# Layer 0's feed-forward up half on one Trainium2 core: seven block products in place of eight, with some of the weights' sums made by DMA

## The chip, the cores and the metric

The kernel runs on one core of one Trainium2 chip. The metric is the device time of one execution in microseconds (us); three runs were timed, and their median counts. A further execution was recorded by the hardware profiler, and the trace is of that one.

## The reference

A diffusion backbone of two layers over 512 latent tokens (x) and 256 context tokens (ctx), model width 1024. Layer 0 mixes tokens by retention, layer 1 by differential attention; each is followed by a gated feed-forward with a convolution of three taps along the tokens. All is float32. Cut to what matters here:

```python
def rms_norm(x, g):
    y = x * lax.rsqrt(jnp.mean(x * x, axis=-1, keepdims=True) + EPS)
    return y * g

def modulate(xn, shift, scale):
    return xn * (1 + scale) + shift

def dwconv3(x, w, b):
    xp = jnp.pad(x, ((0, 0), (1, 1), (0, 0)))
    return xp[:, :-2] * w[0] + xp[:, 1:-1] * w[1] + xp[:, 2:] * w[2] + b

def conv_ffn(u, w_up, conv_w, conv_b, w_down):
    val, gate = jnp.split(u @ w_up, 2, axis=-1)
    return (jax.nn.silu(dwconv3(gate, conv_w, conv_b)) * val) @ w_down

for l in range(DEPTH):
    ...
    h_x = h_x + gm * rms_norm(yx, norm_g[l, 1])
    fx = conv_ffn(modulate(rms_norm(h_x, norm_g[l, 2]), shf, scf),
                  ffn_w_up[l], ffn_conv_w[l], ffn_conv_b[l], ffn_w_down[l])
    h_x = h_x + gf * rms_norm(fx, norm_g[l, 3])
    if not last:
        h_c = h_c + cgm * rms_norm(yc, norm_g[l, 1])
        fc = conv_ffn(modulate(rms_norm(h_c, norm_g[l, 2]), cshf, cscf), ...)
        h_c = h_c + cgf * rms_norm(fc, norm_g[l, 3])
```

The hidden width is 2816, or NF = 22 tiles of 128 (written f); `w_up` therefore has 44 units of 1024 x 128, two per f (gate and value). The shifts, scales and gates (adaLN) come from `silu(c) @ ada_w + ada_b`.

## The kernel before, in words

**Arithmetic.** Every fp32 product of the projections is made from three fp32r matmuls. An operand is split into a high part H (ScalarE copies it with rounding, L59) and a low part L (VectorE subtracts, L60); `split` is the function of both. `mm3` issues H by H, H by L and L by H on one PSUM bank (L97 to L99).

**Weights.** `W` loads a unit of 128x1024 by SP into one of three `wraw` buffers (`load_raw`, L64) and splits it into `wH`, `wL` (two buffers each) or into slots of the pools s2 or s6. The splits of weights and of loaded left operands run under `high_priority(offset=AHEAD)`: the scheduler that orders VectorE, ScalarE and POOL sets them ahead of work that was written up to 300 instructions earlier. SP and PE keep the order in which the code is written (`manual_schedule`).

**Pools.** s2: 48 slots of 128x512; s6: 8 slots of 128x1536; t2: 6 slots of 128x512 for short-lived tiles.

**Stages around the change.** Retention goes head by head: features of q and k (`feat`), projections of v and the gates (`proj_tok`), the two scans, and the result, transposed, goes to the DRAM tensor `yTd` by POOL's queue (`y_out`). `sublayer_out` then makes the output projection `ret_out` with 16 units k. Its **x half** takes tokens 0 to 3: per k SP loads the weights and 128x512 of `yTd`, and TensorE does 24 matmuls of 512 columns (4 tokens, 2 column halves, 3 products). Its **context half** takes tokens 4 and 5: 12 matmuls per k with weights loaded again up to two k ahead (`ahead`). Beside them a table `side` puts work at chosen k's: `fin` (gate, residual: L271, L274, tiles `ft` and `hn`), `keep` (store to DRAM), `sc` (the norm: `rstd_of` on ScalarE and POOL, then `xn` on VectorE), `tr` (16 transposes on TensorE, modulation and split into the operand `u` of the feed-forward, class `UT`).

**The up half** (`FFNUp`): per f, gate and value are each 8 k x 3 matmuls of 512 columns for x and as many of 256 for the context, that is 96 matmuls. `u` is the moving operand, the weights the stationary one. `conv` (L307 on) takes gate and value from PSUM: ScalarE scales and biases, VectorE adds the two neighbours (L323, L325), ScalarE does SiLU, VectorE multiplies by the value (L328). The hidden result stays in SBUF (`hTx`, `hTc`). Tiles 0 and 1 run their x parts first, since the context's tokens are done last:

```python
    F.run(0, 0, "x")
    F.run(0, 1, "x")
    ctx_part()
    F.run(1, 0, "x")
    ...
    F.rest(2)
```

**adaLN units.** 80 units (`ada_unit`): SP loads 128x1024 into `wraw`, VectorE does one or two multiply-reduces over it (L164). Nine per head lie in retention, two or three in a group (36); 44 lie in the up half, one behind each weight unit (`between`).

**The down half** is `sublayer_out` again, with 22 units and operands from SBUF. Layer 1 follows with the same pools.

## Time and profile before

| | |
|---|---|
| median of 3 runs | 2204.94 us (2198.9 to 2206.59) |
| profiled execution, its own time | 2202.28 us |
| its span in the trace | 2200.5 us |
| mean granted TensorE clock | 0.989 |
| TensorE (PE) busy | 2146.4 us, 98% of the span |
| VectorE (DVE) busy | 1222.3 us, 56% |
| ScalarE (ACT) busy | 843.8 us, 38% |
| GpSimd (POOL) busy | 242.5 us, 11% |
| DMA, mean | 114 GB/s |

Times in the trace are us from the span's start unless marked ns. PE is TensorE's matmul side, PEld its weight loads, which overlap. The ends of matmuls are modelled, so one matmul's shown duration overlaps the next; distances of starts tell what one costs. The runs' own time is 1.8 us above the span in the profiled execution. The up half of layer 0 lies between 876 and 1246 us, the x half of `ret_out` between 748 and 831, its context half from there to 877.

### The profile page before, as it was taken

What the parts mean: (1) busy time and instruction counts of PE and PEld (TensorE: products, weight loads), DVE (VectorE), ACT (ScalarE), POOL (GpSimd) and SP (SyncE); (2) the same over time, 40 slices, a digit from 0 to 9 for tenths busy, and PEclk for the clock granted to TensorE, in tenths of its full rate; (3) what the DMA queues carried; (4) which work ended last, traced back from release to release, by engine and by line L of the source; (5) the groups of instructions that cost most, each with busy time, mean ns of one, the idle gap of its engine ahead of it and who ended that gap; (6) DMA issues with size and microseconds to landing.
All of it is one profiled execution on the core that took longest, in us unless ns stands there. A gap on an engine that the chain in (4) does not pass through costs nothing. (4 is left out here: it accounts for less than half of the span.)

```text
span 2200.5 us, 28121 instructions
## 1 busy us (share of the span) xinstructions
PE 2146.4 (98%) x11096; PEld 1825.0 (83%) x11096; DVE 1222.3 (56%) x1923; ACT 843.8 (38%) x1488; POOL 242.5 (11%) x309
## 2 busy tenths in 40 slices
...
GB/s 269 100 92 87 130 86 68 121 86 67 101 96 101 115 220 200 140 116 143 129 124 128 146 105 196 212 44 47 43 45 30 115 114 117 98 99 98 108 96 125
DMA packets 82732, 250.68 MB, mean 114 GB/s; under 512 B 10104, under 2 KB 13480, under 8 KB 82472
## 3 DMA queue, kind: packets, MB, share of 16 engines
...
## 5 line engine op out<-in xcount | busy, mean ns | idle before, releaser
L60 DVE TENSOR_TENSOR wL<-wraw,wH 128x1024 fp32r<-128x1024 f32 x232 | 286.0, 1233 | 504.3 <-ACT wH L59 502.3
L59 ACT ACTIVATE wH<-wraw 128x1024 fp32r<-128x1024 f32 x257 | 271.5, 1058 | 646.1 <-PE psa L99 183.1
L97 PE MATMUL psf<-uxH,wH 128*128 128x512 f32 (+1 forms) x672 | 258.6, 385 | 0.0
L98 PE MATMUL psf<-uxL,wH 128*128 128x512 f32 (+1 forms) x672 | 258.5, 385 | 0.0
L99 PE MATMUL psf<-uxH,wL 128*128 128x512 f32 (+1 forms) x672 | 258.1, 384 | 0.1
L97 PE MATMUL pso<-wH,lxH 128*128 128x512 f32 x432 | 168.3, 390 | 0.5 <-ACT yo L579 0.3
L98 PE MATMUL pso<-wL,lxH 128*128 128x512 f32 x432 | 168.1, 389 | 0.0
L99 PE MATMUL pso<-wH,lxL 128*128 128x512 f32 x432 | 168.1, 389 | 0.0
L99 PEld LDWEIGHTS psf<-uxH,wL 128*128 128x128 f32 x672 | 126.3, 188 | 25.4 <-DVE wL L60 0.3
L97 PEld LDWEIGHTS psf<-uxH,wH 128*128 128x128 f32 x672 | 126.5, 188 | 24.0
L164 DVE CUSTOM_DVE_ANT_0 wraw<-wraw,cb 128x1024 f32<-128x1024 f32 x80 | 97.5, 1222 | 87.5 <-DMA wraw<-in_ada_rest_dram 86.8
L98 PEld LDWEIGHTS psf<-uxL,wH 128*128 128x128 f32 x672 | 126.5, 188 | 23.4
L97 PE MATMUL psa<-wH,uxH 128*128 128x512 f32 x352 | 137.0, 389 | 0.0
L98 PE MATMUL psa<-wL,uxH 128*128 128x512 f32 x352 | 137.0, 389 | 0.0
L99 PE MATMUL psa<-wH,uxL 128*128 128x512 f32 x352 | 136.9, 389 | 0.0
L137 POOL TENSOR_SCALAR st<-st 128x1 f32<-128x1 f32 x42 | 28.7, 684 | 682.3 <-ACT junk L136 681.1
L97 PEld LDWEIGHTS pso<-wH,lxH 128*128 128x128 f32 x432 | 81.1, 188 | 17.8 <-ACT grow L183 0.5
L99 PEld LDWEIGHTS pso<-wH,lxL 128*128 128x128 f32 x432 | 81.1, 188 | 17.0
L99 PE MATMUL psf<-ucH,wL 128*128 128x256 f32 x336 | 95.1, 283 | 0.0
L98 PE MATMUL psf<-ucL,wH 128*128 128x256 f32 x336 | 95.1, 283 | 0.0
L98 PEld LDWEIGHTS pso<-wL,lxH 128*128 128x128 f32 x432 | 81.1, 188 | 16.6
L97 PE MATMUL psf<-ucH,wH 128*128 128x256 f32 x336 | 94.9, 282 | 0.0
...
## 6 DMA issues: line engine op xcount, KB each, us to landing
wraw<-in_up_dram SPq DMA_DIRECT2D x88, 512.0 KB, 3.6
wraw<-in_ada_rest_dram SPq DMA_DIRECT2D x80, 512.0 KB, 3.7
wraw<-in_down_dram SPq DMA_DIRECT2D x66, 512.0 KB, 3.6
wraw<-in_ret_in_dram SPq DMA_DIRECT2D x64, 512.0 KB, 3.7
wraw<-in_ret_out_dram SPq DMA_DIRECT2D x32, 512.0 KB, 3.7
wraw<-in_diff_in_dram SPq DMA_DIRECT2D x24, 512.0 KB, 3.6
wraw<-in_ada_dram SPq DMA_DIRECT2D x16, 512.0 KB, 7.1
wraw<-in_diff_out_dram SPq DMA_DIRECT2D x16, 512.0 KB, 3.7
```

Source lines behind the costliest of these rows:

```text
L59: nc.scalar.activation(out=h, in_=x, func=AF.Copy)
L60: (eng or nc.vector).tensor_tensor(out=l, in0=x, in1=h.bitcast(F32), op=ALU.subtract)
L97: nc.tensor.matmul(ps, l[0], r[0], start=first, stop=False)
L98: nc.tensor.matmul(ps, l[0], r[1], start=False, stop=False)
L99: nc.tensor.matmul(ps, l[1], r[0], start=False, stop=last)
L137: nc.gpsimd.tensor_scalar(out=s[:, 2:3], in0=s[:, 0:1], scalar1=s[:, 1:2], scalar2=EPS, op0=ALU.add, op1=ALU.add)
L164: nc.vector.tensor_tensor_reduce(out=o, in0=raw, in1=cb[:, v, :], scale=1.0, scalar=0.0, op0=ALU.mult, op1=ALU.add, accum_out=adaF[:, laye ...
```

## The change

**Seven block products.** The product of the weights (gate and value; upper and lower half of the model width) with `u` (upper and lower half of the model width; even and odd blocks of 128 tokens) is a 2x2 by 2x2 block product. `seven_pass` makes it of seven block products in the order 1, 6, 7, 5, 2, 4, 3, each 4 k x 3 matmuls of 384 columns (256 of x, 128 of the context): 84 matmuls per f. Products 2, 3 and 4 have no bank of their own: their matmuls go on accumulating (`start=False`) on the banks of 1, 5 and 7. Between them ScalarE copies bank 1 to `p1`, and VectorE makes `u2` = bank 6 + p1, `u3` = bank 7 + u2, and from the banks of 5, 4 and 3 the value and the gate (L929). Tiles 0 and 1 are four passes: x of 0 and 1 (256 columns), then `ctx_part`, then the context of 0 and 1 (128 columns).

**Sums of the weights.** Each product needs its own stationary operand. `seven_load(f)` loads value's and gate's units; `sa` gets, by a plain DMA of SP, the upper halves of both, and then POOL's queue adds the value unit onto it in a DMA with `accum_op=add` (L901). It is issued two tiles ahead. `seven_w(f)` makes two further sums `sb` on VectorE (L912, L915) and splits seven operands (`wH`, `wL`, `opH`, `opL`), one tile ahead, under high priority.

**Sums of u.** Class `Seven` replaces `UT` there: `x_part(q)` (transposes, modulation, four sums and seven splits of 512 columns) at k = 6, 8, 10 and 12 of the context half; `ctx_part` the same for the context after tile 0's and 1's x passes. `seven_load` for tiles 0 and 1 is issued at k = 13, `seven_w(0)` at k = 14.

**The rest.** The hidden result goes to a DRAM tensor `hd` by POOL's queue and is loaded back in the down half (`load_y`), whose first two k's are loaded during tile 21. The adaLN units move: one behind every weight unit of `proj_tok` and every `feat` in retention (60), and the remaining 20 two ahead of each of the first ten k's of the x half of `ret_out`; none lies in the up half. s2 has 31 slots instead of 48, s6 16 instead of 8, and some tiles change pool.

```diff
-        return sp.tile(list(shape), dt, tag="s2", name=name, bufs=48)
+        return sp.tile(list(shape), dt, tag="s2", name=name, bufs=31)
...
-        return sp.tile(list(shape), dt, tag="s6", name=name, bufs=8)
+        return sp.tile(list(shape), dt, tag="s6", name=name, bufs=16)
...
@@ proj_tok, and after feat in retention
+            ada_next(1)
...
@@ retention
-            ada_next(2)
...
-        ada_next(3)
...
-        ada_next(2)
...
@@ sublayer_out
         for k in range(nk - 2):
-            w, lt = W(unit(k)), lx(k)
+            if seven:
+                ada_next(2)
+            w, lt = begun[k] if k < len(begun) else (W(unit(k)), lx(k))
...
-                    wcs.append(W(unit(j), "s6" if j % 2 == 0 else False))
+                    wcs.append(W(unit(j), j % 3 == 2 if seven else "s6" if j % 2 == 0 else False))
...
+        if seven:
+            side[13] = early
+            side |= {6 + 2 * q: lambda q=q: u.x_part(q, xn) for q in range(4)}
...
-            if k == nk - 1:
+            if k == nk - (2 if seven else 1):
                 first = pre()
...
+    ORDER = (1, 6, 7, 5, 2, 4, 3)
+    class Seven:
...
+        def sums(self, lo1, hi1, lo2, hi2, T, at):
+            a, b, c, d = T
+            stt = nc.vector.scalar_tensor_tensor
+            sub(a, lo1, hi1)
+            sub(b, hi2, hi1)
+            stt(out=c, in0=hi2, scalar=-1.0, in1=a, op0=ALU.mult, op1=ALU.subtract)
+            stt(out=d, in0=c, scalar=-1.0, in1=lo2, op0=ALU.mult, op1=ALU.subtract)
+            for i, x in ((1, lo1), (6, c), (7, b), (5, a), (2, lo2), (4, d), (3, hi2)):
+                split(at(self.H[i]), at(self.L[i]), x)
...
+    def seven_load(f):
...
+        nc.sync.dma_start(out=sa.rearrange("p (u c) -> p u c", u=2),
+                          in_=up[2 * f : 2 * f + 2, :, :512].rearrange("u p c -> p u c"))
+        g = load_raw(up[2 * f])
+        nc.sync.dma_start(out=v2, in_=up[2 * f + 1, :, 512:])
+        with tc.high_priority(offset=AHEAD):
+            nc.gpsimd.dma_start(out=sa, in_=up[2 * f + 1], accum_op=ALU.add)
...
+    def seven_w(loaded):
+        g, sa, v2 = loaded
+        with tc.high_priority(offset=AHEAD):
...
+            nc.vector.tensor_tensor(out=sb[0], in0=g[:, :512], in1=sa[:, 512:], op=ALU.add)
+            for i, x in ((6, sb[0]), (7, sa[:, :512]), (5, sa[:, 512:]), (4, v2), (3, sb[1])):
+                if i == 3:
+                    nc.vector.tensor_tensor(out=sb[1], in0=g[:, 512:], in1=sb[0], op=ALU.add)
+                H, L = s2(F32R, name="opH"), s2(F32R, name="opL")
+                split(H, L, x)
+                ops[i] = H, L
...
+    def seven_pass(f, u, ops, p, fp, after):
...
+        for i in ORDER:
+            on = {2: 1, 3: 5, 4: 7}.get(i)
+            banks[i] = banks[on] if on else bank("psf")[:, o]
+            ps = banks[i]
...
+            for k in range(4):
...
+                    nc.tensor.matmul(ps, a, b, start=on is None and k == 0 and j == 0, stop=k == 3 and j == 2,
+                                     skip_group_check=on is not None)
+            if i == 1:
+                after()
...
+        nc.gpsimd.dma_start(out=hd[f, :, s], in_=c[:, s])
...
+        seven_pass(0, u, ops[0], "x", fp, lambda: prepare(1))
+        seven_pass(1, u, ops[1], "x", fp, lambda: more(2))
+        ctx_part()
+        seven_pass(0, u, ops[0], "c", fp, lambda: None)
+        seven_pass(1, u, ops[1], "c", fp, lambda: (prepare(2), more(3)))
+        for f in range(2, NF):
+            seven_pass(f, u, ops[f], "all", fp, lambda: (prepare(f + 1), more(f + 2)))
```

**Where the order changes: VectorE and ScalarE at the start of the up half.** Before, VectorE, from the splits of the first up weights to the context's modulation (`ft`, `hn` and `xn` are tokens 4 and 5; `uf` and `ucL` the context's operand):

```order
L60 TENSOR_TENSOR wlL<-wraw,wlH 128x512 x4
L271 TENSOR_TENSOR ft<-pso,G 128x512 x3
L274 SCALAR_TENSOR_TENSOR hn<-ft,st,hin 128x512 x2
L271 TENSOR_TENSOR ft<-pso,G 128x512
L274 SCALAR_TENSOR_TENSOR hn<-ft,st,hin 128x512 x2
L220 TENSOR_SCALAR xn<-hn,st 128x512 x4
L60 TENSOR_TENSOR wL<-wraw,wH 128x1024 x2
L232 TENSOR_SCALAR uf<-pst,adaF 128x256
L60 TENSOR_TENSOR ucL<-uf,ucH 128x256
L232 TENSOR_SCALAR uf<-pst,adaF 128x256
L60 TENSOR_TENSOR ucL<-uf,ucH 128x256 x2
L232 TENSOR_SCALAR uf<-pst,adaF 128x256
```

After, VectorE at the same place, from the last two operands of tile 0 (`v_7241` is its `v2`; `sb`, `sa` and `v_7248` below `xn` are tile 1's; `u_7448` is pass 0's u2):

```order
L60 TENSOR_TENSOR opL<-v_7241,opH 128x512
L915 TENSOR_TENSOR sb<-wraw,sb 128x512
L60 TENSOR_TENSOR opL<-sb,opH 128x512
L277 SCALAR_TENSOR_TENSOR hn<-ft,st,hin 128x512 x4
L219 TENSOR_SCALAR xn<-hn,st 128x512 x4
L912 TENSOR_TENSOR sb<-wraw,sa 128x512
L60 TENSOR_TENSOR opL<-sb,opH 128x512
L60 TENSOR_TENSOR opL<-sa,opH 128x512 x2
L60 TENSOR_TENSOR opL<-v_7248,opH 128x512
L915 TENSOR_TENSOR sb<-wraw,sb 128x512
L60 TENSOR_TENSOR opL<-sb,opH 128x512
L929 TENSOR_TENSOR u_7448<-psf,p_7433 128x256
```

And ScalarE there in the change (`junk` is the square of the norm, `p_7433` pass 0's p1):

```order
L59 ACTIVATE opH<-sb 128x512
L59 ACTIVATE opH<-sa 128x512 x2
L59 ACTIVATE opH<-v_7241 128x512
L59 ACTIVATE opH<-sb 128x512
L136 ACTIVATE junk,st<-hn 128x512 x4
L183 ACTIVATE grow<-psg 8x128 x2
L59 ACTIVATE opH<-sb 128x512
L59 ACTIVATE opH<-sa 128x512 x2
L59 ACTIVATE opH<-v_7248 128x512
L59 ACTIVATE opH<-sb 128x512
L944 ACTIVATE p_7433<-psf 128x256
```

Tile 1's operands stand ahead of u2 on VectorE and ahead of p1 on ScalarE. On POOL the adding DMA of tile 2 (L901) stands ahead of two of the four steps (L137, L138) of tokens 4's and 5's norm.

**SP in the x half of `ret_out`.** Before, from the last units of retention (`G` is the gate row):

```order
L64 DMA wraw<-in_ret_in_dram 128x1024 x4
L64 DMA wraw<-in_ada_rest_dram 128x1024 x2
L191 DMA G<-gd 128x512 x2
L64 DMA wraw<-in_ret_out_dram 128x1024
L726 DMA yin<-yTd 128x512
L64 DMA wraw<-in_ret_out_dram 128x1024
L726 DMA yin<-yTd 128x512
```

After, from the last units of retention to the second k:

```order
L64 DMA wraw<-in_ret_in_dram 128x1024
L64 DMA wraw<-in_ada_rest_dram 128x1024
L191 DMA G<-gd 128x512 x2
L64 DMA wraw<-in_ada_rest_dram 128x1024 x2
L64 DMA wraw<-in_ret_out_dram 128x1024
L727 DMA yin<-yTd 128x512
L64 DMA wraw<-in_ada_rest_dram 128x1024 x2
L64 DMA wraw<-in_ret_out_dram 128x1024
L727 DMA yin<-yTd 128x512
```

Two adaLN loads now stand ahead of each k's weights, and the single ones lie between the weights of retention.

**VectorE in a steady pass** (f = 3 and later). Before, from one f's gate weights (the two L164 rows are an adaLN unit):

```order
L60 TENSOR_TENSOR wL<-wraw,wH 128x1024
L323 SCALAR_TENSOR_TENSOR conv<-psf,cw,conv 128x511
L325 SCALAR_TENSOR_TENSOR conv<-psf,cw,conv 128x511
L164 ISA adaj,adaF<-wraw,cb 128x1024
L164 ISA adaF 128x1
L164 ISA wraw,adaF<-wraw,cb 128x1024
L164 ISA adaF 128x1
L60 TENSOR_TENSOR wL<-wraw,wH 128x1024
L323 SCALAR_TENSOR_TENSOR conv<-psf,cw,conv 128x255
L325 SCALAR_TENSOR_TENSOR conv<-psf,cw,conv 128x255
L164 ISA adaj,adaF<-wraw,cb 128x1024
L164 ISA adaF 128x1
```

After, from u2 (`u_8009`) and u3 (`u_8024`) of a pass to its gate (`sb`, `sa`, `opL`, `wL` are the next tile's operands):

```order
L929 TENSOR_TENSOR u_8009<-psf,p_7994 128x384
L929 TENSOR_TENSOR u_8024<-psf,u_8009 128x384
L912 TENSOR_TENSOR sb<-wraw,sa 128x512
L60 TENSOR_TENSOR opL<-sb,opH 128x512
L929 TENSOR_TENSOR val<-psf,u_8024 128x3x128
L60 TENSOR_TENSOR opL<-sa,opH 128x512 x2
L60 TENSOR_TENSOR opL<-v_7988,opH 128x512
L915 TENSOR_TENSOR sb<-wraw,sb 128x512
L60 TENSOR_TENSOR wL<-wraw,wH 128x1024
L929 TENSOR_TENSOR val<-psf,u_8009 128x3x128
L60 TENSOR_TENSOR opL<-sb,opH 128x512
L929 TENSOR_TENSOR gate_8053<-psf,u_8009 128x3x128
```

The two adds for the value and the one for the gate stand among the next tile's splits; the adaLN units are gone from here.

## Rows read from the trace of the kernel before

**Rows 1.** The page: busy time, share of the span and instructions.
```profile
PE 2146.4 (98%) x11096; PEld 1825.0 (83%) x11096; DVE 1222.3 (56%) x1923; ACT 843.8 (38%) x1488; POOL 242.5 (11%) x309
```

**Rows 2.** Windows: us, then PE, PEld, DVE, ACT, POOL, PEclk, DMA share, GB/s.
```profile
831.00:877.00 46.00, 45.09 (x216) 37.14 (x215) 35.20 (x64) 31.15 (x67) 6.74 (x8) 1.00 0.61 208
...
905.00:1230.00 325.00, 325.00 (x1873) 287.66 (x1872) 175.58 (x273) 83.21 (x118) 0.00 (x0) 1.00 0.41 130
```

**Rows 3.** Tile psf: count, ns min/median/max, first and last start.
```profile
L97 PE MATMUL psf<-uxH,wlH x80: 277/283/474, 876.6 to 1861.2; 128*128 128x256 f32 x64, 128*128 128x512 f32 x16
...
L99 PE MATMUL psf<-ucH,wL x336: 283/283/283, 900.8 to 1245.3; 128*128 128x256 f32 x168
```

**Rows 4.** Timeline of PE: start us, duration us, instruction.
```profile
995.21 0.40 PE L97 MATMUL psf<-uxH,wH 128*128 128x512 f32 x1
...
1000.68 0.28 PE L97 MATMUL psf<-ucH,wH 128*128 128x256 f32 x1
...
1003.55 0.40 PE L97 MATMUL psf<-uxH,wH 128*128 128x512 f32 x1
```

**Rows 5.** Timeline of VectorE in the x half's end.
```profile
819.49 1.22 DVE L60 TENSOR_TENSOR wlL<-wraw,wlH 128x1024 fp32r<-128x1024 f32 x1
820.62 0.42 DVE L60 TENSOR_TENSOR lcHL<-yin,lcHL 128x256 fp32r<-128x256 f32 x1
820.96 1.28 DVE L271 TENSOR_TENSOR ft<-pso,G 128x512 f32<-128x512 f32 x2
822.16 1.40 DVE L274 SCALAR_TENSOR_TENSOR hn<-ft,st,hin 128x512 f32<-128x512 f32 x2
823.48 1.28 DVE L271 TENSOR_TENSOR ft<-pso,G 128x512 f32<-128x512 f32 x2
```

**Rows 6.** Timeline of ScalarE in the x half.
```profile
757.41 1.06 ACT L59 ACTIVATE wH<-wraw 128x1024 fp32r<-128x1024 f32 x1 [3.68 <-PE pso L99]
758.38 0.61 ACT L59 ACTIVATE lxH<-yin 128x512 fp32r<-128x512 f32 x1
```

**Rows 7.** DMA issues: tile, queue, count, KB, median us to landing; third row from 5 to 60 us.
```profile
wraw<-in_ret_out_dram SPq DMA_DIRECT2D x32, 512.0 KB, 3.7
...
yTd<-yo POOLq DMA_DIRECT2D x16, 256.0 KB, 4.8
...
wraw<-in_ada_dram SPq DMA_DIRECT2D x14, 512.0 KB, 7.8
```

**Rows 8.** Timeline of PE: transposes in the context half, plain fp32 at the start.
```profile
841.54 1.91 PE L242 MATMUL pst<-ident,hn 128*128 128x128 f32 x16
843.21 0.48 PE L97 MATMUL pso<-wH,lcHL 128*128 128x512 f32 x1
...
1.11 5.29 PE L424 MATMUL warm<-ones 128*128 128x128 f32 x26 [1.11 <-DVE etile L125]
6.33 1.89 PE L381 MATMUL psada<-wraw,csil 128*2 128x256 f32 x8
```

**Rows 9.** Timeline of VectorE at the start of the up half.
```profile
876.25 1.88 DVE L271 TENSOR_TENSOR ft<-pso,G 128x512 f32<-128x512 f32 x3
...
884.38 0.88 DVE L220 TENSOR_SCALAR xn<-hn,st 128x512 f32<-128x512 f32 x2 [1.35 <-POOL st L138]
```

**Rows 10.** Windows around an idle stretch of PE in layer 1.
```profile
1725.00:1730.00 5.00, 0.65 (x2) 0.58 (x3) 4.81 (x11) 1.76 (x5) 0.00 (x0) 0.50 0.55 157
1730.00:1735.00 5.00, 5.00 (x23) 4.22 (x22) 0.59 (x2) 1.06 (x1) 0.55 (x1) 0.73 0.00 0
```

**Rows 11.** Timeline of SP in the context half.
```profile
857.48 0.33 SPq L64 DMA_DIRECT2D wraw<-in_ret_out_dram  x1
...
863.69 0.33 SPq L64 DMA_DIRECT2D wraw<-in_ret_out_dram  x1
```

More of the change, by code (lines that the diff above doesn't have):

```diff
@@ L357, in lhs_c @@
         return at
+    cbs = tc.tile_pool(name="cbs", bufs=1)
+    cb = cbs.__enter__().tile([P, 2, 1024], F32, name="cb")
     l0 = tc.tile_pool(name="l0", bufs=1)
@@ L481, in first_ctx @@
     def first_ctx():
-        U.add_ctx()
         norm_pair(psp, U, "c", xs[4:6], 0, 0)
@@ L720, in tile_hybrid_backbone, with load_y @@
         prev_y = yg
-    def load_y(lo, hi):
+    def load_y(src, lo, hi):
         def at(k):
             y = s2(name="yin")
-            nc.sync.dma_start(out=y[:, : hi - lo], in_=yTd[k, :, lo:hi])
+            nc.sync.dma_start(out=y[:, : hi - lo], in_=src[k, :, lo:hi])
             return y[:, : hi - lo]
@@ L730, in tile_hybrid_backbone, with sublayer_out @@
     rows = lambda a, t: a[t * P : (t + 1) * P, :]
-    def sublayer_out(nk, unit, lx, lc, chunk, prev, dst_x, dst_c, layer, sub_i, hook, pre):
+    def sublayer_out(nk, unit, lx, lc, chunk, prev, dst_x, dst_c, layer, sub_i, hook, pre, seven=False, early=None, begun=()):
         G = load_gate(0, chunk, 0)
@@ new lines, in modulated_on @@
+    def modulated_on(uf, ps, k, v, act):
+        a, b = adaF[:, 0, v, 4, k : k + 1], adaF[:, 0, v, 3, k : k + 1]
+        if act:
+            nc.scalar.activation(out=uf, in_=ps, func=AF.Identity, scale=a, bias=b)
+        else:
+            nc.vector.tensor_scalar(out=uf, in0=ps, scalar1=a, scalar2=b, op0=ALU.mult, op1=ALU.add)
+    def seven_load(f):
+        up = A["up"][0]
+        sa = s6(name="sa")[:, :1024]
+        v2 = s2(name="v2")
+        nc.sync.dma_start(out=sa.rearrange("p (u c) -> p u c", u=2),
[4 more added lines that the diff above has]
+            nc.gpsimd.dma_start(out=sa, in_=up[2 * f + 1], accum_op=ALU.add)
+        return g, sa, v2
@@ new lines, in seven_w @@
+    def seven_w(loaded):
+        g, sa, v2 = loaded
+        with tc.high_priority(offset=AHEAD):
+            H, L = wp.tile([P, 1024], F32R, tag="wH", name="wH", bufs=2), wp.tile([P, 1024], F32R, tag="wL", name="wL", bufs=2)
+            split(H, L, g)
+            ops = {1: (H[:, :512], L[:, :512]), 2: (H[:, 512:], L[:, 512:])}
+            sb = [s2(name="sb") for _ in range(2)]
+            nc.vector.tensor_tensor(out=sb[0], in0=g[:, :512], in1=sa[:, 512:], op=ALU.add)
[5 more added lines that the diff above has]
+                ops[i] = H, L
+        return ops
@@ new lines, in ffn0, with more, prepare @@
+    def ffn0(u, loads, ops, ctx_part, then):
+        pool = tc.tile_pool(name="ff", bufs=1)
+        fp = pool.__enter__()
+        end = []
+        def more(f):
+            if f < NF:
+                loads.append(seven_load(f))
+        def prepare(f):
+            if f < NF:
+                ops.append(seven_w(loads[f]))
+            else:
+                end.extend(then())
+        seven_pass(0, u, ops[0], "x", fp, lambda: prepare(1))
[5 more added lines that the diff above has]
+            seven_pass(f, u, ops[f], "all", fp, lambda: (prepare(f + 1), more(f + 2)))
+        pool.__exit__(None, None, None)
+        return end
@@ L818, in tile_hybrid_backbone @@
+    hd = dr.tile([NF, P, 768], F32, name="hd")
+    loads = []
     u, ctx_part, first = sublayer_out(
-        16, lambda k: A["ret_out"][k], lhs_x(load_y(0, 512)), lhs_c(load_y(512, 768)), 2, tok_src,
-        lambda t: rows(h1d, t), lambda t: rows(h1d, t), 0, 1, lambda: y_out(3, prev_y), pre_up)
+        16, lambda k: A["ret_out"][k], lhs_x(load_y(yTd, 0, 512)), lhs_c(load_y(yTd, 512, 768)), 2, tok_src,
+        lambda t: rows(h1d, t), lambda t: rows(h1d, t), 0, 1, lambda: y_out(3, prev_y), lambda: seven_w(loads[0]), True,
+        lambda: loads.extend(seven_load(f) for f in range(2)))
@@ L821, in tile_hybrid_backbone @@
     flush_rows(psp)
-    F = FFNUp(psp, u, 0, True, ada_next)
-    F.w[0, 0], F.w[0, 1] = first
-    F.run(0, 0, "x")
-    F.run(0, 1, "x")
-    ctx_part()
-    F.run(1, 0, "x")
-    F.conv(0, "x")
-    F.run(0, 0, "c")
-    F.run(0, 1, "c")
-    F.run(1, 0, "c")
-    F.conv(0, "c")
-    for p in ("x", "c"):
-        F.run(1, 1, p)
-    F.conv(1, "x")
-    F.conv(1, "c")
-    F.rest(2)
+    l0.__exit__(None, None, None)
+    down, hx = lambda k: A["down"][0, k], lhs_x(load_y(hd, 0, 512))
+    begun = ffn0(u, loads, [first], ctx_part, lambda: [(W(down(0)), hx(0)), (W(down(1), True), hx(1))])
@@ L1052, in part @@
                 yield
-    acc = {}
+    acc, acct = {}, {}
     def evac(t, n, ps):
-        acc[t, n] = s2(name="acc")
+        if t not in acct:
+            acct[t] = s6(shape=(P, 3, 512), name="acc")
+        acc[t, n] = acct[t][:, n, :]
         with tc.high_priority(offset=20):
```

139 lines of the change are left out of this document (109 added, 30 removed).

## The prediction

> **What bounds the kernel now.** I read the page's busy times first: TensorE is busy for 2146.4 of 2200.5 us [rows 1], so the kernel ends when its matmuls are through. Then the windows by stage [rows 2]: in the stretch of layer 0's up half (905 to 1230) TensorE is busy throughout, VectorE 175.58 of 325 us, at full clock; nothing but TensorE can be made shorter there. The tile view of `psf` gives the stage's ends, 876.6 and 1245.3 [rows 3]: 368.7 us. The matmuls overlap, so their price is the distance of their starts: 24 of 512 columns take 5.47 us (995.21 to 1000.68), 24 of 256 take 2.87 (1000.68 to 1003.55) [rows 4], that is 0.228 and 0.1196 each. One tile f has 48 of each, 16.68 us; f = 2 to 21 take 333.6, and the stage's first two tiles with the context's transposes the other 35.1.
>
> The profiled execution took 2202.28 us, 2.66 below the median of the three runs (2204.94). The sum is made against 2202.3; the forecast is left at the sum, since one execution cannot say which of the two a new run will be nearer.
>
> **Tiles f = 2 to 21: the gain.** The change takes 7 x 4 x 3 = 84 matmuls of 384 columns in place of 96. No row has 384 columns; the two prices of [rows 4] lie on a straight line of 0.1084 us per 256 columns, so 0.174, with ends 0.1196 and 0.228. I take the middle: 14.60 us a tile, 2.08 less, over 20 tiles **-41.6 us**. (The ends would be 10.0 and 19.2 us a tile; a price that fell on either would break the line that the two points make, so they don't widen the range.)
>
> This holds if VectorE and ScalarE stay ahead. VectorE's prices are distances of starts [rows 5]: 1.13 us for a 128x1024 split, 0.34 for 256 columns, 0.60 for 512 (ft, from PSUM), 0.66 for a three-operand one of 512. Per tile: 7 sums and splits of 512 (4.2), one of 1024 (1.13), 5 adds of 384 from PSUM (2.35, between 0.34 and 0.60 each), four convolution steps (2.1) and the last product of 768 (0.95): 10.7 of 14.6 us. Today it is 175.58/325 of 16.68, or 9.0 us. ScalarE: 1.06 and five times 0.6 [rows 6], two copies, two convolution steps, some 6.8. In the order of instructions the adds that free the banks of products 7 and 5 come before the splits that wait longest; u3 is due when product 4 starts, 10.4 us into a pass, and stands at about 7.6; val's first add is due at 12.5 and stands at about 10. So I cost the shared banks at nothing; VectorE's slack of some 2.5 us covers them.
>
> The sums by DMA: per tile 512 KB plain and 512 KB added, beside 768 KB of weights and 384 KB of `hd`, 2.2 MB in 14.6 us, 155 GB/s where the stretch now moves 130 [rows 2]. No row has an adding DMA. Nearest: POOL's 256 KB stores land in 4.8 us, SP's 512 KB loads in 3.7, in the crowded start 7.8 [rows 7]. Twice the store's, 9.6 us, is my value, 3.7 the low end; there is no row for a high one. It has about 20 us: `sa` of tile f+2 lands at the start of pass f-1 and is first read some 7.6 us into pass f. At nothing.
>
> **Tiles 0 and 1: a loss.** They run as four passes: 84 matmuls of 256 columns twice (10.0 us each), and 84 of 128 twice. For 128 columns the nearest row is the transposes, 16 in 1.67 us, 0.104 each; the dearest is the plain fp32 matmul of the same shape, 26 in 5.22 us, 0.20 [rows 8]. I take 0.104, as the loads of the stationary operand have the same shape in both: 8.8 us a pass (16.9 at the upper end). The Trainium skill (TensorE: Matmul & The Clock Gate, "Back-to-back issue gap") gives about 81 ns per 128-column matmul with its weight load; the 168 would then cost 3.9 us less. The same sentence gives 131 ns for 512 columns, where the rows above show 228, so I go by the rows.
>
> Waits come on top. Count from the end of the context's products (876.6 in the trace), in VectorE's order as the fences show it: the last ft at 2 us [rows 9]; tile 0's operands, 7 x 0.60 and twice 0.6 of waiting for ScalarE, to 8; hn to 10.5; xn not before 14, because on POOL the two steps of its rstd stand behind tile 2's adding DMA, that waits for a load (3.7 us) which waits for tile 0's `sa` to be read (at 5.5). Today xn is done 8.7 us after the same point. Then tile 1's operands, to 19.7; only then u2 and u3 of pass 0, to 20.5. Product 2 waits for p1, which ScalarE has behind tile 1's splits, and product 4 for u3; TensorE is through products 1, 6, 7 and 5 by 9, idles about 10 us, and ends pass 0 at 24 instead of 10. Pass 1 ends at 34, the transposes at 36. The context's sums (4 modulations, 4 sums, 7 splits of 512 and pass 1's convolution, 10 us) let product 6 start at 45.5; six products of 1.25 us end at 53, the last pass at 61.8. Today: 35.1. **+27 us** (lower end +10, if the order's waits come out at a third; upper +43 with 0.20 for 128 columns). While TensorE idles the clock may fall: the trace shows 0.50 in 1725 to 1730, in which PE was busy for 0.65 us of 5, and 0.73 in the next 5 [rows 10]. Some 3 us at half speed lose **+2** (0 to 5).
>
> **Output projection of retention, x half.** 20 adaLN units move here, two ahead of each of 10 k's loads on SP. With three `wraw` buffers each k now turns all three, and W(k+1)'s load starts only when W(k) is split. The trace's fastest turn of one buffer is 6.21 us (857.48 to 863.69, two issues between) [rows 11]; from its parts, 3.7 landing, 1.06 and 1.13 splits, 0.3 issue, 6.2 too. TensorE needs a k every 24 x 0.228 = 5.47. Ten times 0.75 less some 3 us that W is ahead at the start: +4.5; with landings slower, since three units of 512 KB and one of 256 KB every 6.2 us are 290 GB/s, a k every 7 us and +12. I take **+7** (0 to 20). The 24 units moved into retention's projections and features cost nothing: one unit beside each W every 8 us is what the up half does today without a stall [rows 2]; if that cover were gone, VectorE would be late with evacuations, not TensorE with columns.
>
> **Output projection, context half.** VectorE gains 4 x (11 x 0.34 + 0.46) = 16.8 for the seven sums, and loses 16 x 0.34 + 8 x 0.45 = 9.0: 7.8 us more, where it is busy for 35.2 of 46 today [rows 2]; with operands that wait for ScalarE between the two splits I take **+5** (0 to 12).
>
> `hd`'s stores (POOL) and its loads back (SP, 256 KB beside 512 KB per k) are hidden as retention's `yTd` is, in the same loop; without that cover each k would be late by a landing. The changed buffer counts leave layer 1's order nearly as it was: 0 (-5 to +5).
>
> **Sum:** 2202.3 - 41.6 + 27 + 2 + 7 + 5 = 2201.7, say **2202 us**. A measurement of this kernel tells about 0.5% (11 us) from no change: faster is below 2194, slower above 2216.
>
> **Rivals.**
> 1. *The waits at the stage's start are mostly hidden* (faster). For it: TensorE has most of products 1, 6, 7, 5 to run, and the x half may keep its lead through 10 k's. Then start +16, projections +3 together, clock 0: 2180, up to 2192. Against: an in-order VectorE cannot take u2 before tile 1's operands.
> 2. *128-column matmuls cost what plain fp32 ones do* (slower). 168 x (0.20 - 0.104) = +16, and with the x half at 7 us a k another +5: 2223. It decides from 0.19 us each. For it: plain fp32 is the only non-transposing 128-column row; against it, its operands are plain fp32.
> 3. *The adding DMA is late* (slower). Beyond 20 us from issue to landing each pass waits for it; at 25 us that is 5 us a pass, +100: 2300. For it: no row bounds it. The Trainium skill (DMA: Bandwidth & Descriptors, "SWDGE vs HWDGE vs iDMA") says that GpSimd writes such a DMA's descriptors into SBUF, and that VectorE can lock it out meanwhile. By that rule it would be later the busier VectorE is; no row here shows POOL's DMAs beside a VectorE busy at 73%.
> 4. *The change saves no columns*: 84 matmuls at 0.228 would be 19.2 us a tile, +52: 2295. Both prices of [rows 4] speak against it; a chance within that of case 3.
>
> **Chances.** Forecast 0.35, rival 1 0.33, rival 2 0.27, rivals 3 and 4 0.05. Faster 0.33, same 0.35, slower 0.32. The cases reach from 2180 to 2223; with the ends of the terms beside them and no more than 0.2 left out, the range is 2178 to 2235. The forecast's own range is 2192 to 2214.
>
> **What would show it.** Right: in the middle of the stage 84 matmul starts about 0.174 us apart and a pass of 14.6 us; one idle stretch of TensorE of about 10 us just after the context's products, ended by ScalarE's p1 or VectorE's u3, and one before product 6 of the first context pass; k's of 6.2 us in the first ten of the x half, with the two splits of W as releasers. Wrong: passes longer than 15 us with an `sa` DMA as releaser (rival 3); 128-column starts 0.2 apart (rival 2); no idle stretch above 5 us at the stage's start (rival 1); or new waits in layer 1.

## The result: 1.4% slower, and where the time went

The changed kernel takes 2233.56 us (2231.60 to 2234.95, four runs) against 2204.53 us of the kernel before: a ratio of 1.0136, interval 1.0120 to 1.0151. The forecast was 2202, no change. The profiled execution took 2231.60 us. The first lines of the profile's page, to be read beside [rows 1]:

```profile
span 2229.8 us, 28616 instructions
PE 2139.8 (96%) x11000; PEld 1854.1 (83%) x11000; DVE 1355.4 (61%) x2180; ACT 905.0 (41%) x1588; POOL 283.1 (13%) x354
```

TensorE has 96 matmuls less and 6.6 us less busy time, yet the span is 29.3 us longer: it now stands idle or runs slowly somewhere. The windows by stage say where (us, then PE, PEld, DVE, ACT, POOL, PEclk, DMA share, GB/s). Before, the x half and tiles 0 and 1 ([rows 2] has the context half and the later tiles):

```profile
736.60:827.90 91.30, 90.48 (x409) 74.61 (x408) 38.43 (x49) 35.04 (x55) 7.71 (x16) 1.00 0.58 196
...
876.60:911.70 35.10, 35.10 (x211) 31.23 (x209) 24.71 (x45) 16.45 (x38) 6.35 (x10) 1.00 0.40 136
```

After, in order: x half of the output projection, its context half, pass 0, pass 1, the two context passes, tile 2, tiles 3 to 20.

```profile
741.20:844.50 103.30, 95.50 (x409) 76.08 (x408) 59.56 (x88) 36.39 (x59) 8.56 (x16) 0.97 0.77 261
844.50:894.40 49.90, 48.12 (x226) 39.15 (x225) 47.34 (x95) 37.78 (x85) 14.70 (x11) 1.00 0.76 247
894.50:925.00 30.50, 14.71 (x86) 14.09 (x85) 19.38 (x34) 11.89 (x28) 7.51 (x12) 0.72 0.60 177
925.00:939.10 14.10, 12.06 (x102) 11.82 (x101) 7.26 (x14) 5.50 (x11) 1.52 (x2) 1.00 0.37 85
939.10:961.70 22.60, 18.44 (x84) 18.07 (x85) 14.48 (x26) 8.25 (x15) 1.43 (x2) 0.53 0.29 93
961.70:979.60 17.90, 17.90 (x86) 17.90 (x86) 8.19 (x16) 5.22 (x10) 1.43 (x2) 0.50 0.45 114
979.70:996.50 16.80, 16.80 (x85) 16.80 (x85) 9.16 (x16) 5.78 (x10) 0.57 (x1) 0.85 0.41 104
996.60:1258.00 261.40, 261.40 (x1510) 261.40 (x1509) 199.21 (x320) 118.78 (x179) 23.98 (x34) 1.00 0.53 148
```

The stages run from the first matmul of one to the first of the next:

| stage | before, us | changed, us | difference | forecast |
|---|---|---|---|---|
| all before the x half | 736.6 | 741.2 | +4.6 | 0 |
| x half of `ret_out` | 91.3 | 103.3 | +12.0 | +7 |
| its context half | 48.7 | 49.9 | +1.2 | +5 |
| tiles 0 and 1 of the up half | 35.1 | 85.2 | +50.1 | +29 (with the clock's +2) |
| tiles 2 to 21 | 333.6 | 293.6 | -40.0 | -41.6 |
| all after the up half | 955.1 | 956.6 | +1.5 | 0 |

**The steady passes came as forecast.** The first matmuls of two neighbouring passes:

```profile
1011.13 0.33 PE L939 MATMUL psf<-tH,wH 128*128 128x384 f32 x1
...
1025.69 0.33 PE L939 MATMUL psf<-tH,wH 128*128 128x384 f32 x1
```

14.56 us for 84 matmuls, 0.1733 each, in each of 19 tiles; VectorE is busy for 199.21/261.40 of that, 11.1 us (10.7 forecast). No pass waits for a bank, a sum or a DMA.

**Pass 0 waits twice.** TensorE's timeline, from the last matmul of product 1 to the first of product 2 (in brackets: idle time before, and what ended it); then VectorE's and ScalarE's rows that stand behind it:

```profile
895.86 0.28 PE L939 MATMUL psf<-tH,wL 128*128 128x256 f32 x1
...
901.54 0.58 PE L939 MATMUL psf<-tH,opH 128*128 128x256 f32 x1 [5.41 <-ACT opH L59]
...
908.01 0.28 PE L939 MATMUL psf<-tH,opL 128*128 128x256 f32 x1
...
918.66 0.58 PE L939 MATMUL psf<-tH,wH 128*128 128x256 f32 x1 [10.38 <-ACT p L944]
```

```profile
898.41 1.23 DVE L60 TENSOR_TENSOR wL<-wraw,wH 128x1024 fp32r<-128x1024 f32 x1 [1.16 <-ACT wH L59]
...
900.15 0.68 DVE L912 TENSOR_TENSOR sb<-wraw,sa 128x512 f32<-128x512 f32 x1
...
912.40 0.88 DVE L219 TENSOR_SCALAR xn<-hn,st 128x512 f32<-128x512 f32 x2 [1.35 <-POOL st L138]
...
913.20 0.68 DVE L912 TENSOR_TENSOR sb<-wraw,sa 128x512 f32<-128x512 f32 x1
...
918.98 0.42 DVE L929 TENSOR_TENSOR u<-psf,p 128x256 f32<-128x256 f32 x1
```

```profile
897.32 1.06 ACT L59 ACTIVATE wH<-wraw 128x1024 fp32r<-128x1024 f32 x1 [1.76 <-DMA wraw<-in_up_dram]
...
900.86 0.63 ACT L59 ACTIVATE opH<-sb 128x512 fp32r<-128x512 f32 x1 [1.91 <-DVE sb L912]
...
917.71 0.63 ACT L59 ACTIVATE opH<-sb 128x512 fp32r<-128x512 f32 x1 [1.60 <-DVE sb L915]
918.24 0.37 ACT L944 ACTIVATE p<-psf 128x256 f32<-128x256 f32 x1
```

Product 6 waits 5.41 us for `opH` of tile 0 (ScalarE 900.86). That stands behind `wH` and `wL` of tile 1 (897.32, 898.41), which waited for tile 1's load. That order is not the whole of it: tile 0's adding DMA, issued at 887.11, took 9.3 us from issue to landing, so its sum, which begins at 900.15, could not have begun before some 896.4. Product 2 waits 10.38 us for p1 (918.24), which stands behind tile 1's operands (the last at 917.71); u2 follows at 918.98, behind tokens 4's and 5's `xn` and tile 1's sum (913.20) and its splits.

**The context passes run at half clock.** In 961.70 to 979.60 TensorE is busy without a gap and yet has a granted clock of 0.50, the 1.2 GHz level; 128 columns cost 0.213 us there:

```profile
961.74 0.41 PE L939 MATMUL psf<-tH,wH 128*128 128x128 f32 x1
961.95 0.41 PE L939 MATMUL psf<-tL,wH 128*128 128x128 f32 x1
```

### The profile page after: what moved, and what is told of

It reads as the page before. It is cut to its first block, busy times and chain, and to the rows that moved or that the text cites. A ratio compares the mean times of both kernels' runs of the same rounds, so it can differ in the third digit from the quotient of the medians.

```text
span 2229.8 us, 28616 instructions
## 1 busy us (share of the span) xinstructions
PE 2139.8 (96%) x11000; PEld 1854.1 (83%) x11000; DVE 1355.4 (61%) x2180; ACT 905.0 (41%) x1588; POOL 283.1 (13%) x354
## 3 DMA queue, kind: packets, MB, share of 16 engines
q0 software_dynamic: 7744, 28.08, 5.1%
## 5 line engine op out<-in xcount | busy, mean ns | idle before, releaser
L97 PE MATMUL psa<-wH,u 128*128 128x512 f32 x528 | 205.7, 390 | 0.4 <-DVE ptmp L659 0.4
L98 PE MATMUL psa<-wL,u 128*128 128x512 f32 x528 | 205.5, 389 | 0.0
L99 PE MATMUL psa<-wH,u 128*128 128x512 f32 x528 | 205.4, 389 | 0.0
L939 PE MATMUL psf<-tH,opH 128*128 128x384 f32 (+2 forms) x480 | 163.3, 340 | 5.4 <-ACT opH L59 5.4
L939 PE MATMUL psf<-tL,opH 128*128 128x384 f32 (+2 forms) x480 | 163.0, 340 | 2.5 <-DVE tL L60 2.5
L939 PE MATMUL psf<-tH,opL 128*128 128x384 f32 (+2 forms) x480 | 163.0, 340 | 0.0
L99 PE MATMUL psf<-u,wL 128*128 128x512 f32 (+1 forms) x336 | 127.4, 379 | 0.2 <-DVE wL L60 0.2
L97 PE MATMUL psf<-u,wH 128*128 128x512 f32 (+1 forms) x336 | 127.3, 379 | 0.0
L98 PE MATMUL psf<-u,wH 128*128 128x512 f32 (+1 forms) x336 | 127.3, 379 | 0.0
L164 DVE CUSTOM_DVE_ANT_0 wraw<-wraw,cb 128x1024 f32<-128x1024 f32 x80 | 97.3, 1219 | 36.7 <-DMA wraw<-in_ada_rest_dram 36.0
L97 PEld LDWEIGHTS psa<-wH,u 128*128 128x128 f32 x528 | 99.1, 188 | 21.6 <-DVE ptmp L659 1.3
L99 PEld LDWEIGHTS psa<-wH,u 128*128 128x128 f32 x528 | 99.1, 188 | 20.6
L98 PEld LDWEIGHTS psa<-wL,u 128*128 128x128 f32 x528 | 99.1, 188 | 20.2
L137 POOL TENSOR_SCALAR st<-st 128x1 f32<-128x1 f32 x42 | 33.2, 790 | 641.2 <-ACT junk L136 639.2
L939 PEld LDWEIGHTS psf<-tH,opH 128*128 128x128 f32 x480 | 97.7, 204 | 5.7 <-ACT opH L59 5.6
```

The source lines that it names most:

```text
L97: nc.tensor.matmul(ps, l[0], r[0], start=first, stop=False)
L98: nc.tensor.matmul(ps, l[0], r[1], start=False, stop=False)
L99: nc.tensor.matmul(ps, l[1], r[0], start=False, stop=last)
L137: nc.gpsimd.tensor_scalar(out=s[:, 2:3], in0=s[:, 0:1], scalar1=s[:, 1:2], scalar2=EPS, op0=ALU.add, op1=ALU.add)
L164: nc.vector.tensor_tensor_reduce(out=o, in0=raw, in1=cb[:, v, :], scale=1.0, scalar=0.0, op0=ALU.mult, op1=ALU.add, accum_out=adaF[:, laye ...
L939: nc.tensor.matmul(ps, a, b, start=on is None and k == 0 and j == 0, stop=k == 3 and j == 2, skip_group_check=on is not None)
```

## The experiments

My theory after the result had three parts: the clock in the context passes, the order on VectorE and ScalarE in pass 0, and the adaLN units in the x half. Kernels that share a stage's instructions still differ by some us in it, so I read each edit in its own stage. Except where an edit is said to be on the kernel before, it is on the changed kernel.

### Narrow matmuls at full clock

```diff
+    CUTS = {8: ((0, 256), (256, 384)), 14: ((0, 128), (128, 256), (256, 384))}
...
-                    nc.tensor.matmul(ps, a, b, ...)
+                    for c0, c1 in CUTS.get(f if p == "all" else None, ((0, n),)):
+                        nc.tensor.matmul(ps[:, c0:c1], a, b[:, c0:c1], ...)
```

> The changed kernel with two tiles cut into narrower matmuls in the middle of the steady stretch, where the granted clock is 1.00: tile 8 does each 384-column matmul as 256 and 128 columns, tile 14 as three of 128. Question: why did the two context passes take 17.9 us where 8.8 were forecast. Theory A (their price belongs to the clock, 0.50 in that stretch; at full clock a 128-column matmul costs half of 0.213): tile 8's pass takes 84 x (0.120 + 0.107) = 19.0 us; tile 14's pass 252 x 0.107 = 27.0 us if the clock stays full in a stream of 128-column matmuls, and up to 53.7 us if such a stream itself lets the granted clock fall to 0.50. Theory B (128 columns cost 0.213 at any clock, what plain fp32 costs): tile 8's pass takes 84 x (0.120 + 0.213) = 28.0 us and tile 14's 53.7 us with the granted clock at 1.00.

Tiles 8 and 14 of this kernel do not sum as the reference does (the pieces of one bank start their sums one by one; that this is why was not tried by itself), so only their time is read. Tile 8's pass took 19.37 us, tile 14's 28.08, from the first row below to the second, and the clock stayed full. Timeline of PE and windows:

```profile
1162.03 0.45 PE L941 MATMUL psf<-tH,wH 128*128 128x128 f32 x3
...
1190.11 0.39 PE L941 MATMUL psf<-tH,wH 128*128 128x384 f32 x1
```

```profile
1165.00:1170.00 5.00, 5.00 (x47) 5.00 (x47) 2.09 (x4) 1.22 (x2) 0.56 (x1) 1.00 0.50 98
...
1185.00:1190.00 5.00, 5.00 (x47) 5.00 (x46) 0.56 (x1) 0.00 (x0) 0.00 (x0) 1.00 0.60 102
```

Theory A holds: 28.08/252 is 0.111 us, about half of 0.213. The price of plain fp32 (0.20, [rows 8]) is not that of 128 columns here. And 28 us of them without a gap, begun at full clock, do not lower it.

### Context passes over 256 columns

```diff
-        o = {"x": slice(0, 256), "c": slice(256, 384), "all": slice(0, 384)}[p]
+        o = {"x": slice(0, 256), "c": slice(128, 384), "all": slice(0, 384)}[p]
...
+            full = banks[i][:, 128:384] if p == "c" else banks[i][:, o]
...
-                    nc.tensor.matmul(ps, a, b, ...)
+                    nc.tensor.matmul(full, a, b, ...)
```

> The changed kernel, the context passes of tiles 0 and 1 computed over 256 columns (128 columns of x again beside the 128 of the context, their results unused), so that no 128-column matmul is left there. If the width of the matmuls is what keeps the clock at 0.50 in that stretch: each matmul 0.120, passes of about 10 us instead of 17.9, tile 2's pass 14.6 instead of 16.9, and some 16 to 18 us less in all, near 2215 us. If the waits before the context passes are what lowers the clock, and the width is not what keeps it low, 256 columns cost 0.213 at that clock too: passes of 17.9 us again, and no change (2232).

The two context passes and tile 2's, in windows:

```profile
942.00:959.50 17.50, 13.54 (x84) 13.00 (x85) 12.39 (x23) 7.69 (x14) 0.55 (x1) 0.71 0.24 67
959.50:969.60 10.10, 10.10 (x86) 10.10 (x85) 7.92 (x17) 5.12 (x10) 1.45 (x2) 1.00 0.54 152
969.70:984.10 14.40, 14.40 (x85) 14.40 (x84) 10.89 (x20) 6.19 (x11) 1.44 (x2) 1.00 0.78 204
```

The waits before are still there (the clock of the first window is 0.71), but the clock comes back, the second pass takes 10.1 us instead of 17.9 and tile 2's 14.6 instead of 16.9. The three passes get 15.2 us shorter (42.2 after 57.4), a little less than the 16 to 18 expected. The total, 2221.99, is 9.6 below the changed kernel's profiled execution, since this run was 3.1 us later at the x half and 2.4 slower from the down half's end to layer 1's up half.

### Tile 1's operands behind pass 0

```diff
-        seven_pass(0, u, ops[0], "x", fp, lambda: prepare(1))
+        seven_pass(0, u, ops[0], "x", fp, lambda: None)
+        ops.append(seven_w(loads[1], 1))
```

(The second argument takes the place of `AHEAD` in its `high_priority`.)

> The changed kernel, tile 1's operands (two sums, seven splits) written behind pass 0 and without priority, so that VectorE has u2 and u3 of pass 0 ahead of them. If the second idle stretch of pass 0 (10.4 us before product 2) is tile 1's operands standing ahead of p1 and u2, p1 follows the norm's squares on ScalarE (about 15 us after the pass's start) and u3 follows xn (about 20 us): pass 0 ends some 5 to 8 us earlier, near 2225 us in all. If the norm of tokens 4 and 5 is what bounds it, or if pass 1 then waits for tile 1's operands instead, it is 0 to 3 us.

TensorE's idle times in pass 0, and VectorE's last `xn` and u2:

```profile
905.41 0.58 PE L939 MATMUL psf<-tH,opH 128*128 128x256 f32 x1 [4.95 <-ACT opH L59]
...
913.92 0.38 PE L939 MATMUL psf<-tH,wH 128*128 128x256 f32 x1 [2.11 <-ACT p L944]
...
917.80 0.38 PE L939 MATMUL psf<-tH,opH 128*128 128x256 f32 x1 [2.19 <-DVE u L929]
```

```profile
916.00 0.88 DVE L219 TENSOR_SCALAR xn<-hn,st 128x512 f32<-128x512 f32 x2 [1.35 <-POOL st L138]
916.80 0.41 DVE L929 TENSOR_TENSOR u<-psf,p 128x256 f32<-128x256 f32 x1
```

Pass 0 takes 22.0 us instead of 30.6, 8.6 less and so just above the 5 to 8 expected; 7.3 us of that are left at tile 2's start (77.9 after 85.2). What binds it then is `xn`, right ahead of u2, and the first wait (4.95 us) is untouched, as `wL` of tile 1 still stands ahead of tile 0's sums. The total was 2236.23, not near 2225: before the stage this run was 4.3 us later, and from the down half's end to layer 1's up half 5.9 us slower, both with the changed kernel's instructions.

### adaLN's last 20 units into the up half

```diff
-            if seven:
-                ada_next(2)
...
-            seven_pass(f, u, ops[f], "all", fp, lambda: (prepare(f + 1), more(f + 2)))
+            seven_pass(f, u, ops[f], "all", fp, lambda: (prepare(f + 1), more(f + 2), ada_next(1)))
```

> The changed kernel without adaLN units in the x half of the output projection; the 20 units (of one multiply-reduce each) go one behind each tile's loads in tiles 2 to 21 of the up half. Theory: the two units a k took the weights' buffers and the DMA, and VectorE's time at the half's start; the half goes from 103.3 us to 91 to 94 us, and the steady passes stay at 14.56 us, since VectorE is busy for 11.1 us of them and gets 1.2 more: near 2221 us. Rival: VectorE has no slack for them, and each pass is up to 1.2 us longer, +24 us, near 2245 us; or the x half's loss lies in hd's or other transfers and stays at 103 us.

The x half, and the steady passes:

```profile
743.90:835.10 91.20, 90.55 (x409) 74.60 (x408) 37.35 (x48) 34.79 (x56) 7.73 (x16) 1.00 0.56 182
986.20:1248.00 261.80, 261.80 (x1513) 261.80 (x1512) 215.67 (x359) 118.64 (x179) 23.96 (x34) 1.00 0.67 183
```

91.2 us, what it was before the change, at full clock; the passes stay at 14.56 us with VectorE busy for 215.67/261.80, 12.0 us of each. Total 2223.01. The units were the x half's loss. In the changed kernel the waits of that half, by engine, show how:

```profile
ACT wH L59 <- DMA wraw<-in_ret_out_dram: 25.6, 5, 6.0
...
PE psy L580 <- DVE gate L720: 2.5, 1, 2.5
```

At its start the transposes of head 3's result (`psy`) wait for VectorE's `gate` (L720), which stands among multiply-reduces (L164):

```profile
747.95 1.21 DVE L164 CUSTOM_DVE_ANT_0 wraw<-wraw,cb 128x1024 f32<-128x1024 f32 x1
...
749.09 0.68 DVE L720 TENSOR_TENSOR gate<-gate 128x512 f32<-128x512 f32 x1
```

The fourth matmul behind the last of the transposes, the first at full clock again, starts at 755.91 us, at 745.64 before; 4.6 of those 10.3 us were lost ahead of the half, 5.7 here. Of the 5.7, some 3.3 are idle time (4.1 us in three waits, 0.8 before) and the rest goes with the clock, 0.50 from 749.8 to 752 and 0.51 from there to 756. The other 6.3 us are the k's, whose weights ScalarE waits for. They are not spread evenly: the first matmuls of neighbouring k's stand 5.44 us apart from the second k to the fifth, as before the change, and 5.72, 8.11, 5.45, 7.07, 6.49 and 6.10 us from there to the eleventh.

### The adding DMA's sums on VectorE

```diff
-        nc.sync.dma_start(out=sa.rearrange("p (u c) -> p u c", u=2),
-                          in_=up[2 * f : 2 * f + 2, :, :512].rearrange("u p c -> p u c"))
...
-            nc.gpsimd.dma_start(out=sa, in_=up[2 * f + 1], accum_op=ALU.add)
+        v = s6(name="sa")[:, :1024]
+        nc.sync.dma_start(out=v, in_=up[2 * f + 1])
...
+            nc.vector.tensor_tensor(out=sa[1], in0=v[:, :512], in1=v[:, 512:], op=ALU.add)
+            nc.vector.tensor_tensor(out=sa[0], in0=g[:, :512], in1=v[:, :512], op=ALU.add)
```

> The changed kernel with the two sums that the adding DMA made put on VectorE (two adds of 512 columns a tile; the value unit is loaded whole, in one plain load, and no DMA adds). Theory: in the steady passes the adding DMA costs nothing and saves nothing, since VectorE is busy for 11.1 of 14.56 us and 1.2 more still fit; passes stay at 14.56 us, and the total is within 5 us of the changed kernel's (2227 to 2236 us). Rival (the DMA sums are what keeps VectorE ahead): the adds make VectorE late for the shared banks, and the passes grow by 0.5 us or more, 2243 us or above.

2234.35 us; 18 passes of 14.56 us, pass 0 30.30. The steady stretch:

```profile
997.80:1259.00 261.20, 261.20 (x1509) 261.20 (x1508) 219.87 (x356) 115.42 (x180) 9.72 (x18) 1.00 0.28 99
```

VectorE is busy for 12.3 us of a pass, and the stretch moves 99 GB/s instead of 148. So in the passes of this kernel the adding DMA neither costs nor saves. Its landing time in the changed kernel is the second row here (median us at the end):

```profile
sa<-in_up_dram SPq DMA_DIRECT2D x22, 512.0 KB, 3.8
sa<-in_up_dram POOLq DMA_DIRECT2D x22, 512.0 KB, 5.6
```

A median of 5.6 us, most of them beside a VectorE busy at 76%, against 3.8 for the plain one; the longest was the 9.3 us of tile 0. Rival 3, which needs more than 20, is out. The rule of the Trainium skill that I weighed there (DMA: Bandwidth & Descriptors, "SWDGE vs HWDGE vs iDMA") may hold, but it shows in no pass.

### All three repairs

Besides the edits above, the norm of tokens 4 and 5 comes after pass 0, and the context's transposes after four products of pass 1:

```diff
+        seven_pass(0, u, ops[0], "x", fp, lambda: None)
+        ops.append(seven_w(loads[1], 1))
+        u.norm()
+        seven_pass(1, u, ops[1], "x", fp, lambda: more(2), ctx_part)
```

> All three repairs on the changed kernel, sums by DMA as there: adaLN's 20 units in tiles 2 to 21, context passes over 256 columns, tile 1's operands behind pass 0; besides, the norm of tokens 4 and 5 comes after pass 0, and the context's transposes stand after four products of pass 1. If the three causes found are the loss, their gains add: 2231.6 - 12.1 (x half) - 15.2 (width) - 7 to 15 (order) = 2189 to 2197 us, from the context's last product to tile 2's start some 55 to 62 us instead of 85.2; faster than the kernel before by 0.3 to 0.7%. If one wait only gives way to the next (the context's sums on VectorE, which now do other work as well), that stretch stays above 65 us and the total above 2200.

2185.02 us (2184.01 to 2186.11, four runs) against 2201.57 of the kernel before: ratio 0.9926, interval 0.9909 to 0.9942. The four passes of tiles 0 and 1:

```profile
879.50:896.50 17.00, 12.68 (x87) 12.23 (x86) 14.86 (x27) 10.64 (x26) 5.74 (x10) 0.80 0.78 209
896.50:908.30 11.80, 11.80 (x102) 11.80 (x101) 11.70 (x24) 7.59 (x15) 1.54 (x2) 1.00 0.58 184
908.30:922.50 14.20, 11.77 (x86) 11.57 (x85) 11.10 (x21) 6.16 (x11) 0.58 (x1) 0.88 0.43 118
922.50:932.60 10.10, 10.10 (x86) 10.10 (x85) 7.92 (x17) 5.12 (x10) 1.48 (x2) 1.00 0.49 173
```

53.2 us to tile 2's start instead of 85.2, below the 55 to 62 expected. The context passes over 256 columns and the moved operands had taken 13.0 and 7.3 us off that stretch when run alone. The other 11.8 come with the later norm and the earlier transposes, or with the repairs together; no run parts these. Two waits are left: 4.32 us for tile 0's `opH` in pass 0 and 2.43 us for a context split in the first context pass.

With the sums on VectorE in addition:

> As the run with all three repairs, and the sums on VectorE in place of the adding DMA. Theory: at the start of the stage tile 0's operands no longer wait for a load and then an adding DMA behind it, but VectorE has 1.2 us more for each of the two tiles; the total is within 5 us of the run with all three repairs, either way. Rival: with adaLN's unit as well VectorE is busy for 13.5 us of each pass and falls behind: passes above 14.8 us, 5 us or more slower than that run.

2191.62 us, 6.6 slower than without; ratio to before 0.9956 (0.9941 to 0.9970). The passes did not grow (14.56 us), and the up half took 345.5 us instead of 344.2. The two profiled executions differ by 11.2 us, most of it where both kernels do the same work: 5.1 us are there at the x half's start, 4.3 from the down half's end to layer 1's up half (two executions of the kernel before differ by 3.8 in that stretch). So it doesn't tell against sums on VectorE, and its cause stays open.

### The repairs with 128 columns in the context passes

> As the run with all three repairs, but with the context passes of 128 columns as in the change. Question: is it the width by itself, or the width behind a wait, that costs. A matmul of 128 columns takes 0.111 at full clock, less than 0.120 for 256. If the clock stays full, the two context passes take 9.4 us each beside their waits, and the total is 1 us below that run (2184). If the wait of some 3 us before the second product of the first context pass, which stands in that run too, lowers the clock and the narrow matmuls then keep it at 0.50, both passes take 17.9 us and more and tile 2's pass up to 16.9: 2200 to 2204 us.

2199.24 us, 14.2 above the run with 256. Windows over the end of pass 1, the two context passes and tile 2:

```profile
907.00:913.00 6.00, 5.33 (x46) 5.19 (x45) 6.00 (x13) 4.35 (x9) 0.89 (x1) 1.00 0.57 124
913.00:930.00 17.00, 15.09 (x76) 15.09 (x76) 11.17 (x21) 5.93 (x11) 1.43 (x2) 0.59 0.45 141
930.00:949.00 19.00, 19.00 (x87) 19.00 (x87) 10.05 (x20) 5.67 (x11) 1.43 (x2) 0.50 0.48 130
949.00:965.00 16.00, 16.00 (x90) 16.00 (x90) 8.70 (x15) 6.21 (x10) 1.41 (x2) 0.96 0.53 149
```

The second case holds: one wait of 2.58 us, within the second product of the first context pass, and from some 1 us behind it the clock is at 0.50 to the end of both passes (18.30 and 17.92 us), until the 384-column matmuls of tile 2 bring it back. In the run with 256 columns the same wait (2.43 us) lowered the clock too, to 0.88 over that pass, and it was back within the pass.

### The first part: adaLN's early slots, a second profile, adaLN's places

```diff
-            wada[k, kh] = W(A["ada0"][k * 2 + kh], late=("s6" if kh == 0 else True) if k % 2 == 1 else False, ...)
+            wada[k, kh] = W(A["ada0"][k * 2 + kh], late=k % 2 == 1, ...)
```

> The changed kernel with the weights of layer 0's first adaLN products (the start, before 72 us) in the slots that they had before the change, four s2 slots for a unit and none of s6. The x half of retention's output projection starts at 736.6 us in the kernel before and at 739.3 to 745.1 in eight kernels that share the change's first part, most of it lost by 72 us. If those slots are the cause, the x half starts at about 737 to 739 us here and the total is some 4 us below the changed kernel's (2228). If the loss is in the adaLN units that lie elsewhere in retention, in the operand's own slots, or in the spread of one execution to another, it starts at 740 or later.

It started at 744.98 us: not the slots. The total, 2245.23, is 13.6 above the changed kernel's: besides the later start, the x half took 109.7 us, where five other kernels with the units there took 103.2 to 104.2, and the stretch from the down half's end to layer 1's up half 5.6 more. Why is open. The kernel before was then profiled again, and run with the change's places of adaLN's units in retention (the `ada_next` edits of the change, on the kernel before):

> The kernel before, unchanged, profiled a second time, to see how far one execution's first part differs from another's. The x half of the output projection started at 736.6 us in the first profile of it; if executions spread as the nine kernels that share the change's first part do (739.3 to 745.1), it starts anywhere from 734 to 740 here, and part of the change's 4.6 us is spread; if it starts within 1 us of 736.6, the change's first part does cost 3 to 8 us.

> The kernel before with its adaLN units in retention where the change has them (one behind each feature's context part and one behind each weight unit of the projections, 60 in all), the other 20 one behind each of the first weight units of the up half. If those places are what the first part loses, the x half starts at 740 us or later and the total is 3 to 6 us above the kernel before; if not, it starts where the second profile of the kernel before does, within 2 us, and the total is the same within 3 us.

The first matmul of the x half in the second profile of the kernel before, and in that with the units moved:

```profile
737.20 0.39 PE L97 MATMUL pso<-wH,lxH 128*128 128x512 f32 x1
```

```profile
739.55 0.39 PE L97 MATMUL pso<-wH,lxH 128*128 128x512 f32 x1
```

The kernel before repeats within 0.6 us, so the change's first part loses, as far as two executions can show. The units' places account for some 2.3 us of it, by one execution each, between the two cases that I had set (within 2 us, or 740 us and later). The total is 2207.73, ratio 1.0014 (1.0004 to 1.0024); as much again as in the first part is lost in the up half. The other 0 to 6 us, most of them lost by 72 us, where neither adaLN's places nor its slots tell anything, stay open.

## Why the prediction was wrong

The forecast was no change, and the kernel became slower. The profiled 2231.6 us lie near the upper end of the stated 2178 to 2235, and outside the forecast's own 2192 to 2214.

**Step by step.**

- *Tiles 2 to 21*: right, 14.56 for 14.60 us; the price on the line between 256 and 512 columns was 0.1733 for 0.174 (the table's -40.0 has tile 2's loss in it, below). The shared banks and the adding DMA cost nothing there, as costed. Two slips in the working change nothing: the DMA's 2.2 MB in 14.6 us are 153 GB/s and not 155 (148 were measured), and rival 4's +52 is +50 by its own prices.
- *Order at the stage's start*: right in kind. The two waits came where the fences put them, released by tile 0's operands and p1, 15.8 us together for some 14. The long one is the 10 us forecast; the first, 5.4 us, is some 4 in the working and missing among the signs. Of some 8 us of waiting ahead of the context's product 6 and in it, 6.2 came, in three waits.
- *128 columns at 0.104*: near, for full clock (0.111). *The clock, +2 (0 to 5)*: **this is the step that failed.** At half clock the 168 matmuls cost 0.213 instead of 0.111, 17.1 us; tile 2's pass lost 2.4, and some 40 matmuls of 256 columns behind the two waits of pass 0, at 0.213 instead of 0.120 for most, some 4: 23.5 us. The stage's start cost +52.5 (50.1 and tile 2's 2.4) for a forecast of +29; the clock is 21.5 of the difference, and of the other 2 the price of 0.111 for 0.104 is 1.2. I had taken the clock from one row ([rows 10]) in which it came back within 10 us, and priced a short dip; I did not ask what the engine would run behind the wait.
- *x half*: +12.0 in a range of 0 to 20, for +7. The k's cost 6.3 us, between the 4.5 and 12 worked out from the turn of three buffers, but in five of the ten k's and not as an even 6.2 us. VectorE's lateness for head 3's transposes, 5.7 us, was not in the sum; that the range held is partly its width.
- *Context half*: +1.2 for +5, in its range.
- *Units moved into retention at nothing*: off, some +2.3 by one execution on the kernel before.

Rival 2 named nearly the right price, 0.20 for 0.213, and the wrong cause: it made the operand's type the reason and missed that tile 2 and pass 0 would pay too. By the forecast's own terms, with the clock as measured (+23.5 for +2), the sum would have been 2223. The x half's 5 us, the first part's 4.6 and those other 2, less the 3.8 that the context half did not take, bring it to 2231; the execution took 2231.6.

**The clock again.** In the changed kernel TensorE ran five products of the first context pass and all of the second, 30 us, without a gap and at half clock. The Trainium skill (TensorE: Matmul & The Clock Gate, "HAM oscillation — how this bites in real kernels") describes short bursts of matmuls between waits, each of which begins at the slow clock again. The falls agree with the rows here (0.213 us for 256 columns behind the waits of 5.41 and 10.38 us in pass 0). The Trainium skill also has activity release the clock (TensorE: Matmul & The Clock Gate, "What's actually happening"). The rows here agree for 256 and 384 columns, with which it came back; in 30 us of 128-column matmuls without a gap it did not.
